# A decoder layer on one core: cheaper form of LayerNorm's column steps, modulated copies on ScalarE, the second modulation and gate both summed inside attention, and the first LayerNorm's scaling moved ahead

## The chip, the cores and the metric

The kernel runs on one core of one Trainium2 chip. Its engines are TensorE (PE: products and transposes), VectorE (DVE), ScalarE (ACT), GpSimd (POOL) and SyncE (SP, which here issues all loads and stores). The metric is device time in microseconds (us), from the first to the last instruction of one execution; lower is better.

## The reference

One transformer layer on 1024 tokens of 1024 features, all float32 with products of split operands. What is computed, cut to what matters:

```python
mod = silu(c) @ w_mod + b_mod        # shift1, scale1, gate1, shift2, scale2, gate2: 1024 each
h   = x * (1 + scale1) + shift1
q, k, v, u, iq, ik, iw = split(h @ w_in)          # 8 heads of 64, 512 pooling channels, an indexer
score = einsum(iw, relu(iq . ik)); keep the 256 best keys of each query (causal)
attn  = softmax over the kept keys (rotary q, k) @ v
pool  = (mean over the last 2/4/8/16 tokens - u) @ w_pool * pool_scale
x = layer_norm(ALPHA * x + gate1 * (concat(attn, pool) @ w_o), ln1_g, ln1_b)
h = x * (1 + scale2) + shift2
x = layer_norm(ALPHA * x + gate2 * ((silu(h @ w_gate) * (h @ w_up)) @ w_down), ln2_g, ln2_b)
```

`w_up`, `w_gate` are 1024 x 2816, `w_down` 2816 x 1024. The first LayerNorm's result is needed twice: scaled and shifted by `ln1_g`, `ln1_b` as the residual of the second, and folded with the second modulation as the feed-forward's input.

## The kernel before

Tokens are cut into eight tiles of 128, held with tokens on partitions; features are cut into eight tiles as well. Products run as three products of float32r halves (`SPLITS`), so every operand is split once into a rounded part and a rest.

The stages, with their times in the profile: first modulation, h transposed and index queries (0 to 75 us); token index scores (75 to 165); the top-256 threshold of each query, found by a search over the bits of its scores, on DVE for tiles 7, 6, 5 and on ACT and POOL for 4, 3, 2, beside the projections of u, k and v (165 to 405); attention in 32 units, a unit being a pair of heads and a query tile, later queries first (to 537); the loads and splits of the output weights with the output projection (532 to 635); residual, LayerNorm 1 and the operands of the feed-forward (575 to 660); the feed-forward, whose gate and up products are done by blocks after Winograd (635 to 1290); the last down product with LayerNorm 2 and the stores (to the end).

Instructions are recorded through `Queue` (line 121). While an engine's name is in `pinned`, its instructions keep the order in which they were written; before attention `pinned` is cleared (line 940), and from there on a scheduler may put an instruction of DVE, ACT or POOL ahead of others, as its operands allow. All instructions of engines have the helper's line, 157, in the profile, and all loads line 154, so everything below goes by the names of tiles: a buffer's name and the area of SBUF in which it lies (`modraw_V`, `stat_C`, `res_X`).

What the change touches:

- `mods()` (lines 445 to 468) makes the second modulation's scale and shift per feature: sixteen dot products of a 128x1024 block of `w_mod` (`modraw_V`, three slots in area V) with silu(c) (`srow_V`), each one DVE instruction (`CUSTOM_DVE_ANT_0 modraw_V<-modraw_V,srow_V` in the profile, followed by a row that reads its accumulator). A generator, it is stepped once per unit from unit 4 on, and its instructions may be moved by the scheduler. Its results `h2c` are first needed by `region_t`, after LayerNorm 1.
- `gate_acc` (line 426) sums a gate over eight blocks of `w_mod`, one DVE step each: a TENSOR_SCALAR, then seven SCALAR_TENSOR_TENSOR of 128x1024. It is used for the first gate at the start of the program, and for the second beside the output projection, where the sum is kept in `GR` (`gr_G`) and the blocks come through two slots of area R, three steps after each tile's LayerNorm. Two products with a matrix of ones then sum over partitions (`gt`), ACT copies them back into `GR`, and POOL adds the bias `brow`.
- `layer_norm_tile` (line 1150): statistics, then on single columns (128x1, `stat_C`) four TENSOR_SCALAR for the start of an inverse square root, and three Newton steps of two SCALAR_TENSOR_TENSOR each; in LayerNorm 1 a seventh for the shift `nm`, and ACT normalises. LayerNorm 2 (tail) calls it with `affine`: DVE or ACT and then POOL scale and shift the 1024 columns; POOL does it for all but the last tile.
- `region_t` (line 1200): transposes of a normalized tile on PE, and from their PSUM eight modulated copies of 128x128 into `stage_W`: the first four on DVE, the others on ACT.
- `affine` (line 1435): with `lnb` (gain and bias of LayerNorm 1, spread over the partitions), each residual tile is multiplied on DVE and the bias added on DVE or, for tiles 7, 5, 3, 1, on POOL; called once per block product in the first part of the feed-forward.
- `load_set`, `make_block`, `gu_step`, `down` load, build and use the blocks of feed-forward weights (`wraw`, `wblk`); `GR` is used when `make_block` scales blocks of the down weights.

## Time and profile before

| | us |
| --- | --- |
| three runs | 1356.88, 1364.34, 1357.63 (median 1357.63) |
| the profiled execution, first to last instruction | 1357.8 |
| PE busy | 1214.3 (89% of the span) |
| DVE busy | 1082.5 (80%) |
| ACT busy | 544.4 (40%) |
| POOL busy | 608.9 (45%) |
| granted clock of TensorE, mean | 0.951 of full |

The profiled execution's own time is its span, 1357.8 us, and agrees with the median of the runs. An engine's row counts the time in which it works; register, branch and DMA-issuing instructions do not count. A group of instructions of one tile is shown with its count, its busy time, and the mean duration of one; groups can overlap by a little, since an instruction may start before the one ahead has ended. The idle time before an instruction is put down to what released it last. A stretch's row shows each engine's busy time in it, and so which engine is full there, which an average over the whole span does not tell.

### The profile page before, as it was taken

What the parts mean: (1) busy time and instruction counts of PE and PEld (TensorE: products, weight loads), DVE (VectorE), ACT (ScalarE), POOL (GpSimd) and SP (SyncE); (2) the same over time, 40 slices, a digit from 0 to 9 for tenths busy, and PEclk for the clock granted to TensorE, in tenths of its full rate; (3) what the DMA queues carried; (4) which work ended last, traced back from release to release, by engine and by line L of the source; (5) the groups of instructions that cost most, each with busy time, mean ns of one, the idle gap of its engine ahead of it and who ended that gap; (6) DMA issues with size and microseconds to landing.
All of it is one profiled execution on the core that took longest, in us unless ns stands there. A gap on an engine that the chain in (4) does not pass through costs nothing.

```text
span 1357.8 us, 15982 instructions
## 1 busy us (share of the span) xinstructions
PE 1214.3 (89%) x5570; PEld 954.6 (70%) x5570; DVE 1082.5 (80%) x1763; ACT 544.4 (40%) x1019; POOL 608.9 (45%) x629
## 2 busy tenths in 40 slices
PE   7989996767849999997789999999999999999993
PEld 6646575655626666876668888888888888888872
DVE  6898899899999766499997767677676767676788
ACT  3446733553757787236422323132232313232310
POOL 1492774866534445235672415234141523423545
PEclk8989997978868999999899999999999999999997
DMA  9640020312120115520301112010110201011111
GB/s 338 232 146 16 16 93 16 124 47 78 63 70 24 55 40 192 167 76 1 109 31 63 63 41 84 32 63 32 63 63 31 94 32 62 31 63 63 63 47 77
DMA packets 24850, 101.79 MB, mean 75 GB/s; under 512 B 3393, under 2 KB 3393, under 8 KB 20290
## 3 DMA queue, kind: packets, MB, share of 16 engines
q1 hardware_dynamic: 24770, 100.77, 21.2%
q8 instruction: 44, 0.72, 0.2%
q14 instruction: 36, 0.29, 0.1%
HBM read 92.37 MB, written 8.39 MB: 74 GB/s over the span
## 4 chain that ended last, share of the span: by engine, by line
PE 50%; DVE 31%; issue 6%; POOL 5%; ACT 4%; DMA 3%; SPq 0%; DVEq 0%; POOLq 0%; ACTq 0%
PE gu L157 28%; PE dn L157 15%; DVE junk_X L157 6%; DVE stat_C L157 4%; DVE score_X L157 3%; PE s L157 2%; DVE res_X L157 2%; PE o L157 2%; PE pT L157 2%; POOL colsA_X L157 2%; DVE stage_W L157 1%; DVE colsD_X L157 1%; DVE hr_H L157 1%; DVE modraw_V L157 1%; DVE hT_H L157 1%
## 5 line engine op out<-in xcount | busy, mean ns | idle before, releaser
L157 POOL TENSOR_TENSOR wraw_R<-wraw_R 128x512 f32<-128x512 f32 x44 | 60.9, 1384 | 173.5 <-DVE wblk_T L157 52.0
L157 DVE TENSOR_TENSOR res_X<-res_X,dn 128x512 f32<-128x512 f32 (+1 forms) x145 | 97.3, 680 | 49.5 <-PE dn L157 49.5
L157 POOL TENSOR_TENSOR wraw_W<-wraw_W 128x512 f32<-128x512 f32 x44 | 60.5, 1374 | 168.5 <-DVE wblk_V L157 63.1
L157 PE MATMUL gu<-hr_H,wblk_V 128*128 128x512 f32 (+1 forms) x552 | 128.0, 387 | 8.4 <-ACT gtmp_V L157 3.7
L157 PE MATMUL pj<-ws_W,hT_H 128*128 128x512 f32 x456 | 122.1, 416 | 14.3 <-DVE kr_K L157 6.5
L157 PE MATMUL gu<-hr_H,wblk_T 128*128 128x512 f32 (+1 forms) x552 | 126.5, 386 | 4.5 <-ACT stage_W L157 4.5
L157 PE MATMUL gu<-hr_H,wblk_W 128*128 128x512 f32 (+1 forms) x552 | 124.9, 381 | 4.0 <-DVE utmp_X L157 4.0
L157 PEld LDWEIGHTS gu<-hr_H,wblk_V 128*128 128x128 f32 x552 | 102.8, 193 | 30.4 <-ACT gtmp_V L157 3.9
L157 PEld LDWEIGHTS gu<-hr_H,wblk_T 128*128 128x128 f32 x552 | 102.7, 194 | 24.5 <-ACT stage_W L157 4.8
L157 PEld LDWEIGHTS gu<-hr_H,wblk_W 128*128 128x128 f32 x552 | 100.5, 188 | 24.8 <-DVE utmp_X L157 2.8
L157 PEld LDWEIGHTS pj<-ws_W,hT_H 128*128 128x128 f32 x456 | 87.4, 198 | 41.1 <-issue 16.7
L157 DVE TENSOR_TENSOR utmp_X<-utmp_X,gu 128x512 f32<-128x512 f32 x88 | 58.1, 682 | 33.3 <-PE gu L157 32.4
L157 DVE TENSOR_TENSOR gtmp_V<-gtmp_V,gu 128x512 f32<-128x512 f32 (+1 forms) x96 | 59.4, 638 | 26.3 <-PE gu L157 26.2
L157 DVE TENSOR_SCALAR_CACHE_REDUCE junk_X<-keysD_T,colsD_X 128x1024 int16<-128x1024 int16 (+1 forms) x64 | 78.9, 1270 | 0.8
L157 POOL TENSOR_SCALAR sm_H<-sm_H,stat_X 128x1024 f32<-128x1024 f32 (+7 forms) x64 | 51.3, 816 | 62.9 <-DVE stat_X L157 47.5
L157 PE MATMUL dn<-wblk_V,act_W 128*128 128x512 f32 x288 | 75.8, 395 | 2.9 <-DVE res_X L157 2.9
L157 PE MATMUL dn<-wblk_T,act_W 128*128 128x512 f32 (+1 forms) x294 | 75.2, 385 | 2.0 <-DVE res_X L157 2.0
L157 PE MATMUL gu<-hr_H,wblk_R 128*128 128x512 f32 (+1 forms) x276 | 66.7, 391 | 4.0 <-DVE gtmp_V L157 3.4
L157 PEld LDWEIGHTS dn<-wblk_V,act_W 128*128 128x128 f32 x288 | 54.6, 190 | 15.1 <-DVE res_X L157 3.8
L157 PEld LDWEIGHTS dn<-wblk_T,act_W 128*128 128x128 f32 x294 | 54.5, 188 | 13.3 <-DVE res_X L157 2.2
L157 PEld LDWEIGHTS gu<-hr_H,wblk_R 128*128 128x128 f32 x276 | 52.0, 194 | 15.0 <-DVE gtmp_V L157 3.6
L157 PE MATMUL dn<-wblk_W,act_W 128*128 128x512 f32 x240 | 62.2, 389 | 0.0
(287 smaller groups left out, 2834.9 us busy)
## 6 DMA issues: line engine op xcount, KB each, us to landing
wm_K<-in_wma_dram SPq DMA_DIRECT2D x16, 512.0 KB, 9.8
modraw_V<-in_wmc_dram SPq DMA_DIRECT2D x16, 512.0 KB, 3.6
wraw_R<-in_wg_dram SPq DMA_DIRECT2D x6, 1024.0 KB, 4.8
wraw_R<-in_wd_dram SPq DMA_DIRECT2D x6, 1024.0 KB, 4.8
wraw_W<-in_wup_dram SPq DMA_DIRECT2D x6, 1024.0 KB, 4.7
wraw_R<-in_wup_dram SPq DMA_DIRECT2D x5, 1024.0 KB, 4.7
wraw_W<-in_wg_dram SPq DMA_DIRECT2D x5, 1024.0 KB, 4.8
wraw_W<-in_wd_dram SPq DMA_DIRECT2D x5, 1024.0 KB, 4.7
```

Of the source, the lines that this page charges most:

```text
L157: ins_ = f(*a, **k)
```

## The change

1. `mods()` starts at unit 8 and is stepped twice per unit, and its dots go through `kept`, which pins them: they stay where they were written.
2. The second gate is summed at the end of `mods()`, eight more pinned steps in area V, then summed over partitions, joined with its bias on one row and stored to `g2_d`. `GR` holds the gain of LayerNorm 1 in the meantime, and gets the gate from `g2_d` when the last residual tile has been multiplied. The steps beside the output projection, the two `gt` products and copies in the feed-forward and the bias addition on POOL are gone.
3. In `layer_norm_tile` the Newton steps and `nm` become tensor_scalar with two columns as scalars.
4. In `region_t` the first four copies are on DVE only for tiles 1 and 0, else on ACT.
5. The affine multiplications take the gain from `GR`, which is there before LayerNorm 1 ends; `lnb` holds the bias alone. `affine` is called in every second block product of the gate's second half and in five of the up's.

```diff
-MODS = (4, (0, 1, 2, 3))
+MODS = (8, 2)
...
+    g2_d = tc.dram_tile([1, 1024], F32, name="g2_d")
+    def kept(op, *a):
+        own = "V" not in pinned
+        pinned.add("V")
+        getattr(V, op)(*a)
+        if own:
+            pinned.discard("V")
...
-            V.tensor_tensor_reduce(wm, wm, srow2, 1.0, 0.0, ALU.mult, ALU.add, m2[:, u : u + 1])
+            kept("tensor_tensor_reduce", wm, wm, srow2, 1.0, 0.0, ALU.mult, ALU.add, m2[:, u : u + 1])
...
+        acc = buf("V", 4096, 1024, "gacc")
+        wms = []
+        for k in range(3):
+            wms.append(ring[(16 + k) % 3])
+            SP.dma_start(wms[k], wmg_in[1, k])
+        for k in range(KT):
+            if k == 0:
+                kept("tensor_scalar", acc, wms[k], silc[:, 0:1], None, ALU.mult)
+            else:
+                kept("scalar_tensor_tensor", acc, wms[k], silc[:, k : k + 1], acc, ALU.mult, ALU.add)
+            if k + 3 < KT:
+                wms.append(ring[(16 + k + 3) % 3])
+                SP.dma_start(wms[k + 3], wmg_in[1, k + 3])
+            yield
+        grow = buf("V", 5120, 1024, "grow")
+        SP.dma_start(grow[0:1, :], bg_in[1:2, :])
+        for c in range(2):
+            pm = psA("gt")
+            cc = slice(c * 512, (c + 1) * 512)
+            T.matmul(pm, ones, acc[:, cc], start=True, stop=True)
+            V.tensor_tensor(grow[0:1, cc], grow[0:1, cc], pm[0:1, :], ALU.add)
+        SP.dma_start(g2_d, grow[0:1, :])
...
-        if n_ >= MODS[0] and (n_ - MODS[0]) % 4 in MODS[1]:
-            next(mod_steps, None)
+        if n_ >= MODS[0]:
+            for _ in range(MODS[1]):
+                next(mod_steps, None)
...
-            V.scalar_tensor_tensor(a, y, w, y, ALU.mult, ALU.mult)
-            V.scalar_tensor_tensor(y, a, 1.5, y, ALU.add, ALU.mult)
+            V.tensor_scalar(a, y, w, y, ALU.mult, ALU.mult)
+            V.tensor_scalar(y, a, 1.5, y, ALU.add, ALU.mult)
         if affine is None:
-            V.scalar_tensor_tensor(nm, mv[:, 0:1], -1.0, y, ALU.mult, ALU.mult)
+            V.tensor_scalar(nm, mv[:, 0:1], -1.0, y, ALU.mult, ALU.mult)
...
-                if c == 0:
+                if c == 0 and t < 2:
...
-    g2 = gate_acc(1, GR, g2_ring, 1)
+    SP.dma_start(GR, ln_in[0:1, 0:1024].to_broadcast([P, 1024]))
...
-        for _ in range(3):
-            next(g2, None)
...
-    lnb = buf("W", 4096, 2048, "lnb")
-    SP.dma_start(lnb, ln_in[0:1, :].to_broadcast([P, 2048]))
+    lnb = buf("W", 5120, 1024, "lnb")
+    SP.dma_start(lnb, ln_in[0:1, 1024:2048].to_broadcast([P, 1024]))
...
-        if n == 4:
-            for c in range(2):
-                pm = psA("gt")
-                T.matmul(pm, ones, GR[:, c * 512 : (c + 1) * 512], start=True, stop=True)
-                A.activation(GR[:, c * 512 : (c + 1) * 512], pm, AF.Copy)
...
-            V.tensor_tensor(XR[t], XR[t], lnb[:, 0:1024], ALU.mult)
-            (G if t in AFF_G else V).tensor_tensor(XR[t], XR[t], lnb[:, 1024:2048], ALU.add)
+            V.tensor_tensor(XR[t], XR[t], GR, ALU.mult)
+            (G if t in AFF_G else V).tensor_tensor(XR[t], XR[t], lnb, ALU.add)
+            if not todo:
+                SP.dma_start(GR, g2_d.to_broadcast([P, 1024]))
...
-        affine()
-    G.tensor_tensor(GR, GR, brow, ALU.add)
-    gate_up("u", ACTS, lambda n: affine() if n < 4 else None)
+        if n % 2:
+            affine()
+    gate_up("u", ACTS, lambda n: affine() if n < 5 else None)
```

The built order shows where this puts instructions. On DVE in attention, `sm_H` is the masked maximum of a unit's scores `s` (one row, and one that reads its accumulator), `pT_H` a copy of transposed probabilities, `modraw_V` a dot. Before, this is where the last two of the sixteen dots stand, at the units whose key ranges are 640 and 768; fourteen are further ahead, ten of them before the first `sm_H`:

```order
L157 ISA modraw_V_3015,const_C_78<-modraw_V_3015,srow_V_3013 128x1024
L157 ISA const_C_78 128x1
L157 ISA sm_H_2588,stat_X_2583<-s_3137,score_X_77 128x640
L157 ISA stat_X_2583 128x1
L157 ISA sm_H_2588,stat_X_2583<-s_3138,score_X_77 128x640
L157 ISA stat_X_2583 128x1
L157 COPY pT_H_2587<-pT_3171 128x3x128
L157 ISA modraw_V_3014,const_C_78<-modraw_V_3014,srow_V_3013 128x1024
```

After, on DVE at the next unit with 640 keys, the first three of the sixteen:

```order
L157 ISA modraw_V_3221,const_C_78<-modraw_V_3221,srow_V_3220 128x1024
L157 ISA const_C_78 128x1
L157 ISA sm_H_2589,stat_X_2584<-s_3231,score_X_77 128x640
L157 ISA stat_X_2584 128x1
L157 ISA sm_H_2589,stat_X_2584<-s_3232,score_X_77 128x640
L157 ISA stat_X_2584 128x1
L157 COPY pT_H_2586<-pT_3263 128x128
L157 ISA modraw_V_3222,const_C_78<-modraw_V_3222,srow_V_3220 128x1024
L157 ISA const_C_78 128x1
L157 RECIPROCAL stat_X_2584<-stat_X_2584 128x2
L157 ISA modraw_V_3223,const_C_78<-modraw_V_3223,srow_V_3220 128x1024
```

All sixteen now stand here and behind, two for each unit's pair of maxima, and the eight gate steps (`gacc_V`) follow them.

On DVE at the start of LayerNorm 1, before, the last split of pooled channels (`hr_H`), four gate steps through slots of area R, and the first residuals `res_X`:

```order
L157 TENSOR_TENSOR hr_H_2676<-raw_R_75,hr_H_2676 128x3x256
L157 TENSOR_SCALAR gr_G_76<-raw_R_74,const_C_78 128x1024
L157 SCALAR_TENSOR_TENSOR gr_G_76<-raw_R_73,const_C_78,gr_G_76 128x1024
L157 SCALAR_TENSOR_TENSOR gr_G_76<-raw_R_74,const_C_78,gr_G_76 128x1024
L157 SCALAR_TENSOR_TENSOR gr_G_76<-raw_R_73,const_C_78,gr_G_76 128x1024
L157 SCALAR_TENSOR_TENSOR res_X_4053<-res_X_4053,wo_4087 128x512 x2
L157 SCALAR_TENSOR_TENSOR res_X_4052<-res_X_4052,wo_4088 128x512
```

After, at the same place on DVE:

```order
L157 TENSOR_TENSOR hr_H_2677<-raw_R_75,hr_H_2677 128x3x256
L157 TENSOR_TENSOR wblk_R_4094<-wraw_R_4101,wblk_R_4094 128x512
L157 SCALAR_TENSOR_TENSOR res_X_4080<-res_X_4080,wo_4114 128x512 x2
L157 BN_STATS stat_C_4089<-res_X_4080 128x6
L157 SCALAR_TENSOR_TENSOR res_X_4079<-res_X_4079,wo_4115 128x512
```

The gate steps are gone, and the rest of the first block of feed-forward weights, whose load is the first behind those of the pooled channels and of the gain, stands ahead of the residuals.

On SP late in attention, after, loads of the second gate's blocks (`in_wmg`) among loads of output weights (`in_wo`) and of x:

```order
L154 DMA modraw_V_3222<-in_wmg_dram 128x1024
L154 DMA raw_R_74<-in_wo_dram 128x1024
L154 DMA modraw_V_3223<-in_wmg_dram 128x1024
L154 DMA modraw_V_3221<-in_wmg_dram 128x1024
L154 DMA modraw_V_3222<-in_wmg_dram 128x1024
L154 DMA res_X_4078<-in_x_dram 128x1024
L154 DMA modraw_V_3223<-in_wmg_dram 128x1024
```

Before, no load of the second gate stands in attention; on SP they follow the last loads of output weights and pooled channels (`pool_d`), ahead of the feed-forward's first weights; here the first five of the eight:

```order
L154 DMA raw_R_74<-in_wo_dram 128x1024
L154 DMA raw_R_75<-pool_d 128x1024
L154 DMA raw_R_73<-in_wmg_dram 128x1024
L154 DMA raw_R_74<-in_wmg_dram 128x1024 x2
L154 DMA raw_R_73<-in_wmg_dram 128x1024
L154 DMA raw_R_74<-in_wmg_dram 128x1024
```

Eight loads of 512 KB have moved from behind attention into it, two of them behind a load whose target is still in use by attention.

## Rows read from the trace of the kernel before

**Rows 1.** The page: first the line of its part 1 (busy time, share of the span and number of instructions of each engine), then the first line of its part 4 (the chain of work that ended last, by engine).

```profile
PE 1214.3 (89%) x5570; PEld 954.6 (70%) x5570; DVE 1082.5 (80%) x1763; ACT 544.4 (40%) x1019; POOL 608.9 (45%) x629
...
PE 50%; DVE 31%; issue 6%; POOL 5%; ACT 4%; DMA 3%; SPq 0%; DVEq 0%; POOLq 0%; ACTq 0%
```

**Rows 2.** The view of stretches: from and to in us, length, busy time (number of instructions) of PE, PEld, DVE, ACT and POOL, then the granted clock of TensorE, the share of the DMA engines and GB/s. In order: search beside the k projection, the end of the search and the first attention units, attention up to unit 8, attention units 8 to 24, LayerNorm 1, start of the feed-forward, feed-forward, tail.

```profile
290.00:330.00 40.00, 24.36 (x88) 19.27 (x88) 38.99 (x62) 13.53 (x26) 19.08 (x23) 0.79 0.24 79
365.00:405.00 40.00, 21.08 (x86) 15.70 (x84) 39.56 (x83) 22.96 (x50) 19.63 (x48) 0.73 0.26 85
405.00:441.00 36.00, 34.41 (x178) 21.67 (x179) 33.74 (x72) 26.47 (x49) 15.39 (x16) 0.82 0.07 23
441.00:515.00 74.00, 72.63 (x510) 49.66 (x508) 51.86 (x134) 60.06 (x137) 34.96 (x37) 1.00 0.18 56
575.00:640.00 65.00, 59.42 (x294) 48.52 (x292) 61.50 (x158) 29.46 (x55) 26.48 (x18) 1.00 0.13 47
640.00:717.00 77.00, 56.71 (x274) 47.26 (x274) 74.13 (x91) 28.45 (x55) 51.71 (x29) 0.87 0.18 62
717.00:1290.00 573.00, 572.58 (x2525) 473.46 (x2523) 402.29 (x533) 164.12 (x276) 200.14 (x147) 1.00 0.16 56
1290.00:1358.00 68.00, 43.45 (x191) 35.34 (x191) 60.08 (x134) 7.47 (x6) 33.17 (x14) 0.86 0.15 62
```

**Rows 3.** Groups of DVE by tile, 290 to 403 us (before the first masked score of attention): name of the group, count, busy us and mean ns of one, idle time before them; then a row of the timeline of PE (start, duration, engine, in brackets the wait ahead of it and what ended it).

```profile
L157 DVE CUSTOM_DVE_ANT_0 modraw_V<-modraw_V,srow_V 128x1024 f32<-128x1024 f32 x10 | 13.1, 1310 | 0.0
...
401.13 2.46 PE L157 MATMUL s<-kr_K,qab_H 64*128 64x512 f32 x4 [10.98 <-DVE qab_H L157]
```

**Rows 4.** Groups of DVE by tile, 403 to 536 us (attention): the dot products, the split of output weights; a row of the DMA part of the page (loads of modulation weights: count, KB each, median us from issue to landing); timeline of DVE, two steps of the first gate.

```profile
L157 DVE CUSTOM_DVE_ANT_0 modraw_V<-modraw_V,srow_V 128x1024 f32<-128x1024 f32 x6 | 8.4, 1396 | 0.0
L157 DVE TENSOR_TENSOR wo_V<-raw_R,wo_V 128x1024 fp32r<-128x1024 f32 x2 | 3.1, 1537 | 0.0
...
modraw_V<-in_wmc_dram SPq DMA_DIRECT2D x16, 512.0 KB, 3.6
...
85.11 2.30 DVE L157 SCALAR_TENSOR_TENSOR modacc_X<-modraw_V,const_C,modacc_X 128x1024 f32<-128x1024 f32 x1
109.67 1.28 DVE L157 SCALAR_TENSOR_TENSOR modacc_X<-modraw_T,const_C,modacc_X 128x1024 f32<-128x1024 f32 x1
```

**Rows 5.** Timeline of DVE from 563 us, the first step of the second gate and the first residual of LayerNorm 1; then a row of the DMA part of the page (loads of feed-forward weights).

```profile
567.32 0.75 DVE L157 TENSOR_SCALAR gr_G<-raw_R,const_C 128x1024 f32<-128x1024 f32 x1 [2.27 <-DMA raw_R<-in_wmg_dram]
575.36 3.67 DVE L157 SCALAR_TENSOR_TENSOR res_X<-res_X,wo 128x512 f32<-128x512 f32 x6
...
wraw_R<-in_wg_dram SPq DMA_DIRECT2D x6, 1024.0 KB, 4.8
```

**Rows 6.** Groups of DVE by tile, 575 to 640 us, and the last one of ACT in the same stretch.

```profile
L157 DVE SCALAR_TENSOR_TENSOR stat_C<-stat_C 128x1 f32<-128x1 f32 x49 | 11.6, 251 | 0.9
L157 DVE TENSOR_SCALAR stage_W<-xT,const_C 128x128 f32<-128x128 f32 x24 | 8.1, 404 | 0.0
L157 DVE SCALAR_TENSOR_TENSOR gr_G<-raw_R,const_C,gr_G 128x1024 f32<-128x1024 f32 x5 | 6.4, 1280 | 2.5 <-DMA raw_R<-in_wmg_dram 2.5
L157 DVE TENSOR_SCALAR stat_C<-stat_C 128x1 f32<-128x1 f32 (+1 forms) x28 | 3.4, 148 | 0.3
...
L157 ACT ACTIVATE stage_W<-xT,const_C 128x128 f32<-128x128 f32 x24 | 8.8, 456 | 0.0
```

**Rows 7.** Groups of DVE and of POOL by tile, 640 to 717 us; and a row of the timeline of DVE there.

```profile
L157 DVE TENSOR_TENSOR res_X<-res_X,lnb_W 128x1024 f32<-128x1024 f32 x12 | 19.4, 1623 | 0.0
...
L157 POOL TENSOR_TENSOR gr_G<-gr_G,brow_W 128x1024 f32<-128x1024 f32 x1 | 3.3, 3319 | 0.0
...
680.92 1.21 DVE L157 TENSOR_TENSOR res_X<-res_X,lnb_W 128x1024 f32<-128x1024 f32 x1
```

**Rows 8.** The tail. Timeline of DVE for one token tile and the last tile, with the two groups of the column steps over 1290 to 1358 us ahead; then a row of POOL (in brackets its wait), what PE waited for in that stretch (us in total, times, longest), and its last products.

```profile
L157 DVE SCALAR_TENSOR_TENSOR stat_C<-stat_C 128x1 f32<-128x1 f32 x54 | 26.5, 491 | 1.3
L157 DVE TENSOR_SCALAR stat_C<-stat_C 128x1 f32<-128x1 f32 (+1 forms) x32 | 4.0, 149 | 0.6
...
1307.75 0.53 DVE L157 TENSOR_SCALAR stat_C<-stat_C 128x1 f32<-128x1 f32 x4
1308.31 4.08 DVE L157 SCALAR_TENSOR_TENSOR stat_C<-stat_C 128x1 f32<-128x1 f32 x3
1313.63 0.59 DVE L157 SCALAR_TENSOR_TENSOR stat_C<-stat_C 128x1 f32<-128x1 f32 x3
1346.38 0.42 DVE L157 TENSOR_TENSOR res_X<-res_X,dn 128x256 f32<-128x256 f32 x1
...
1307.50 4.87 POOL L157 TENSOR_TENSOR res_X<-res_X,wraw_R 128x1024 f32<-128x1024 f32 x2 [3.21 <-ACT res_X L157]
...
PE dn L157 <- DVE res_X L157: 4.9, 3, 2.3
...
1338.35 0.52 PE L157 MATMUL dn<-hr_H 128*128 128x256 f32 x3
```

**Rows 9.** Timeline of DVE and POOL in the search: a step of three columns, and what POOL did at that time.

```profile
302.00 1.25 DVE L157 TENSOR_SCALAR colsD_X<-colsD_X 128x3 f32<-128x3 f32 x1
...
301.06 2.16 POOL L157 TENSOR_TENSOR rope_V<-rope_V,gr_G 128x512 f32<-128x512 f32 x1
```

More of the change, by code (lines that the diff above doesn't have):

```diff
@@ L1356, in act_op @@
         return q[t % 2][:, o : o + P]
-    n_g = [0]
-    def g2_ring():
-        n_g[0] += 1
-        return RAW[n_g[0] % 2]
     first = {}
@@ L1404, in decoder_layer_kernel @@
             make_block()
-    for _ in g2:
-        pass
     for _ in range(4):
@@ L1430, in decoder_layer_kernel @@
     load_set(2)
-    brow = buf("W", 2048, 1024, "brow")
-    SP.dma_start(brow, bg_in[1:2, :].to_broadcast([P, 1024]))
     todo = list(ORDER)
```

## The prediction

> **What bounds the kernel now.** I read the page first, for who is busy and who ends the chain: PE is busy for 89% of the span, DVE for 80%, but the chain of work that ended last runs through PE for 50% and through DVE for 31% [rows 1]. So neither figure alone says what an edit is worth, and the view of stretches comes next [rows 2]. It splits the program in two kinds. In the feed-forward, 717 to 1290 us, PE is busy 572.58 of 573 us and DVE 402.29: nothing that DVE saves there counts, and work pushed into it is free. Everywhere that this change touches, DVE is the full engine: 38.99 of 40 us and 39.56 of 40 us in the search, 33.74 of 36 in the first part of attention, 61.50 of 65 in LayerNorm 1, 74.13 of 77 at the start of the feed-forward, 60.08 of 68 in the tail. The one exception is attention from unit 8 on, 441 to 515 us: PE 72.63 of 74, DVE 51.86. The change takes DVE work out of the full stretches and puts some of it into that exception. I then read the groups by tile for the size of each piece, and the timelines for what waits.
>
> **A, the search: ten dot products go.** Before, ten of the sixteen `modraw_V` dots of the second modulation run ahead of attention: 10 x 1.310 = 13.1 us on a DVE without gaps [rows 2, 3]. PE is busy there 24.36 and 21.08 of 40 us, and enters attention's scores after a wait of 10.98 us on DVE [rows 2, 3]. Nothing else is late by as much, so nearly all of it should come back; ACT and POOL search tiles 4 to 2 beside it and could hold back a part. Bounds -6 (half, if their search ends last) and -13.1; I take **-11**. Their loads leave this stretch too; its DMA engines are a quarter busy, so I give that nothing.
>
> **B, attention: sixteen dots and eight gate steps come.** One dot leaves 405 to 441 us, five leave 441 to 515, and all sixteen now stand in the latter: net 11 x 1.396 = 15.4 us [rows 4]. The gate adds one step of 0.75 [rows 5] and seven of 1.28 = 9.7 us; one split of output weights that stood here, 1.5 [rows 4], moves behind it. So DVE has 51.86 + 15.4 + 9.7 - 1.5 = 75.4 us of work in a stretch of 74 that PE fills as well. Two engines that wait for each other do not both run at 100%: between 405 and 441 us DVE reached 33.74/36 = 94% [rows 2]. At that share 75.4 us take 80.2, or +6. A gate step beside POOL took 2.30 instead of 1.28 in the first gate [rows 4]; three of seven such cost another 3. I take **+9**, with +1.4 (perfect packing) and +23.6 (all of it in series: 15.4 + 9.7 - 1.5) as ends. The pinned steps also wait for loads, and what is queued behind such a wait on DVE are the masked maxima of the next unit, on which POOL, ACT and PE wait in turn. On SP, two gate loads stand behind a load of x or of output weights that must wait for attention itself. A load lands in 3.6 us [rows 4], a slot of the three comes back every three steps, so 24 steps need 24/3 x (3.6 + 1.4) = 40 us, less than the 74 there are. I count no wait for loads, but keep it in the upper end.
>
> **C, D, E, LayerNorm 1 and the start of the feed-forward.** These are one stretch, since DVE is behind in all of it. C: the first residual starts at 575.36, behind gate steps of which the first waited 2.27 us until 567.32 [rows 5]. In the new order one split of a gate block stands there, whose load of 1024 KB takes 4.8 us [rows 5]; begun at 565.0, where that wait began, and with a copy and a split behind it (an estimate: half of 1.28 each, the gate step of twice the width), it ends near 571.1: DVE starts **4** us earlier. The LayerNorm gain, 512 KB, is issued ahead of that load on SP; where the two share the DMA engines, half of 4.8 us of this is lost again. D: off DVE go the gate steps, 4 x 1.28 = 5.1, the twenty-four modulated copies, 8.1, and of 49 column steps the difference between 251 and 148 ns, 5.0; on come six multiplications at 1.21, 7.3 [rows 6, 7]: **-10.9**. The copies land on ACT, 24 x 0.456 = 10.9 us [rows 6] on an engine busy 29.46 of 65: covered, and if that cover were gone they would cost no more than the 8.1 they save. E: of twelve 1024-wide affine steps, 19.4 us at a mean of 1.62, six are gone [rows 7]: **-9.7**. The addition on POOL (3.32 us) and the two gate copies on ACT go as well; they were beside. Together DVE has some 25 us less of the 142 between 575 and 717: 135.6 of work become 115.0, less than PE's 59.42 + 56.71 = 116.1. So PE is late next, and the gain is not 25. If PE works at the 91% that it has now in LayerNorm 1 (59.42/65), its 116.1 us take 127: **-15**. Ends: -5.6, what PE idles there between 575 and 640, and -25.9, no gap at all.
>
> **F, the tail.** Column steps of one token tile: four TENSOR_SCALAR take 0.53 us at 1307.75 while POOL is in its two multiply-adds (1307.50, 4.87 us); the three SCALAR_TENSOR_TENSOR right behind take 4.08, and three such after POOL is done 0.59 [rows 8]. So one form waits until POOL's instruction ends and the other does not. Over the tail 54 column steps take 26.5 us at 491 ns; at 149 ns, the TENSOR_SCALAR's, they are 8.0: 18.5 us off DVE, whose 60.08 become 41.6 beside PE's 43.45 [rows 2, 8]. PE is next. It waits 4.9 us for DVE's additions, and DVE adds the last piece at 1346.38, some 7.5 us behind PE's last products (1338.35 + 0.52) [rows 8]. If DVE keeps up, 4.9 and nearly all of 7.5 go: **-12**, with -14 as end where the clock (0.86 here) rises as PE's gaps close, and 0 as the other.
> That page of the Trainium skill which speaks of this port, "SBUF — State Buffer", section "Who interferes with whom", says that a DVE instruction with two SBUF inputs contends with a GpSimd one that reads SBUF; by that rule the 4.08 us are the lock, and the trace agrees.
>
> **Sum.** -11 + 9 - 15 - 12 = -29 on a profiled span of 1357.8 us, which is the median of the runs (1357.63): about **1329 us**.
>
> **Rivals.** (1) *The new form waits for POOL as well.* For it: a TENSOR_SCALAR of three columns took 1.25 us at 302.00, inside an instruction of POOL that ran from 301.06 to 303.22 [rows 9]. Against: the four single columns at 1307.75 do not wait, and single columns are what the change writes, though with two pointers for scalars, which those four have not. Then F is 0, and LayerNorm 1, with 5.0 more on DVE and so 120 against PE's 116, loses about 3: 1329 + 12 + 3 = 1344.
> The Trainium skill's "VectorE: DVE Perf Modes", section "The perf-mode tier table (the rule you actually need)", lets float32 tensor_scalar run in a 2x mode in SBUF, and "SBUF — State Buffer", section "Who interferes with whom", says that such modes take the port that GpSimd uses; by these this rival would win, and only the three-column row agrees with it.
> (2) *Attention becomes DVE's.* All that is added lies in series with PE's transposes: B is +23.6, 1329 + 14.6 = 1344. For it: 75.4 us of work in 74. Against: DVE idles 22 us there now. (3) *PE bounds LayerNorm 1.* Its products are as long as before, and only its 5.6 us of gaps up to 640 close: 1329 + 9.4 = 1338. Against: 20 us of gaps from 640 to 717, behind a late DVE. (4) *Slower: the clock falls in attention.* From 441 to 515 us it is granted 1.00; in the two search stretches where PE waits for DVE it was 0.79 and 0.73 [rows 2]. If pinned steps, held by late loads, leave PE such gaps, its 72.63 us take longer: at 0.73 they take 99, which is +25 instead of +9 (1345); the time passes 1364 once the stretch loses 44, that is 72.63/118 = a mean clock of 0.62, below any row shown; at 0.55 it would take 132, and the kernel 1378. What would have to be so for it: most units waiting for a load.
>
> **How the numbers follow.** Forecast 0.50 (1320 to 1337); rival 1 0.13; rival 2 0.13; rival 3 0.12; better than the forecast, with C to E near -25.9, 0.06; rival 4 0.06. Of the mass of rivals 1 and 2, 7 in 100 are both at once, 1358. The range takes rivals 1 to 3 in and a part of the better case: 1312 to 1347. Faster by over 0.5% (about what a measurement of this kernel can tell from no change: 6.8 us), which is below 1351: forecast, better case and most of rivals 1 to 3, 0.87. Within: both rivals at once, or rival 4 at a middling clock, 0.08. Slower: 0.05.
>
> **What would show it.** A: no dot ahead of the first masked score, which starts some 11 us earlier. B: between the same units DVE above 93%, PE's waits on DVE there a few us, clock still 1.00; waits of DVE on modulation loads would speak for rival 4. C to E: first residual near 571 less what A and B leave, PE over 90% up to the steady part. F: three column steps in 0.5 us while POOL runs, a tile every 5 to 6 us instead of 8.1, PE without waits on DVE. If column steps of 2 us remain beside POOL, rival 1 holds. I am wrong as a whole if attention gives back more than 38 us, all that the other parts gain (11 + 15 + 12).

## The result, and the profile after

The changed kernel takes 1339.22 us (median of four runs, 1337.46 to 1342.38) beside 1359.32 for the kernel before on the same chip: the ratio is 0.9856, with a 95% interval of 0.9838 to 0.9874. It is some 20 us faster. The forecast was 1329: the sign held, and the gain is two thirds of what the sum said. The time lies inside the wide range (1312 to 1347), but outside the 1320 to 1337 that had a chance of 0.50. The profiled execution spans 1340.4 us; it is the longest of the four, so the events below add up to 17.9 us and not to 20.

To see where the difference arises, I read the same events in the timelines of both kernels. The table is worked out from their rows: each number is the time of an event in the changed kernel less the time of the same event before.

| event | before, us | after, us | difference | the part of it that arose since the event above | forecast |
| --- | --- | --- | --- | --- | --- |
| first masked maximum on DVE | 403.77 | 397.39 | -6.4 | A: -6.4 | -11 |
| end of attention's last product (`o`) | 536.66 | 553.64 | +17.0 | B: +23.4 | +9 |
| first down product (`dn`) | 728.58 | 725.36 | -3.2 | C to E: -20.2 | -15 |
| end of the last DVE instruction | 1354.69 | 1336.76 | -17.9 | F: -14.7 | -12 |

The forecasts are the terms of the prediction's sum. Two of the three gains went further than the sum had them, A less far, and attention took back 23.4 us instead of 9.

The view of stretches of the changed kernel, in the columns of [rows 2] and at mostly the same times (an event now lies up to 17 us later or earlier in them):

```profile
365.00:405.00 40.00, 23.28 (x75) 16.00 (x76) 37.12 (x75) 22.22 (x47) 11.36 (x30) 0.71 0.07 20
441.00:515.00 74.00, 69.31 (x463) 45.38 (x464) 59.81 (x141) 55.33 (x125) 34.27 (x31) 1.00 0.44 147
515.00:575.00 60.00, 53.57 (x271) 38.08 (x272) 37.83 (x89) 31.78 (x83) 26.30 (x28) 0.89 0.54 187
575.00:640.00 65.00, 64.43 (x309) 53.63 (x308) 47.93 (x131) 33.05 (x67) 24.30 (x17) 1.00 0.08 26
640.00:717.00 77.00, 64.11 (x342) 56.32 (x340) 63.91 (x93) 34.19 (x69) 48.77 (x29) 0.91 0.17 59
1290.00:1340.00 50.00, 38.30 (x181) 32.01 (x179) 42.29 (x131) 7.47 (x6) 33.87 (x14) 0.91 0.21 84
```

LayerNorm 1 has changed its bound: PE is busy 64.43 of 65 us where it was 59.42, and DVE 47.93 where it was 61.50 [rows 2]. The stretch that does not fit is attention: DVE is busy 59.81 of 74 us, not full at all, and yet the end is late. A share of 81% would have passed as slack. What the share hides is seen with shorter stretches (same columns), which also show the granted clock falling; first the changed kernel, then the kernel before in its last units:

```profile
515.00:520.00 5.00, 4.47 (x22) 2.90 (x22) 4.92 (x9) 1.46 (x5) 4.46 (x3) 0.66 0.88 310
520.00:525.00 5.00, 1.19 (x4) 0.67 (x4) 5.00 (x11) 2.70 (x8) 1.36 (x2) 0.68 0.41 157
525.00:530.00 5.00, 4.12 (x7) 1.98 (x8) 3.52 (x9) 2.06 (x6) 1.15 (x2) 0.50 0.82 315
530.00:535.00 5.00, 5.00 (x32) 3.45 (x31) 1.72 (x5) 3.61 (x7) 0.94 (x2) 0.79 0.39 111
535.00:540.00 5.00, 4.75 (x38) 3.50 (x37) 4.58 (x18) 4.46 (x16) 3.53 (x2) 1.00 0.84 316
...
500.00:520.00 20.00, 18.59 (x140) 12.94 (x136) 12.02 (x36) 17.87 (x47) 12.22 (x14) 1.00 0.37 130
520.00:537.00 17.00, 16.27 (x109) 10.56 (x109) 10.10 (x47) 12.86 (x50) 12.20 (x18) 1.00 0.54 193
```

From 520 to 525 us PE does 1.19 us of work in five, and DVE is full. The clock is granted 0.66 from 515 us on and 0.50, the lower of the two levels (1.2 GHz), from 525 to 530; in the kernel before it stays at 1.00 to the end of attention. The timelines of DVE and PE in the same place (start, duration, engine; in brackets the wait and what ended it):

```profile
517.37 1.54 DVE L157 SCALAR_TENSOR_TENSOR gacc_V<-modraw_V,const_C,gacc_V 128x1024 f32<-128x1024 f32 x1
518.94 0.69 DVE L157 CUSTOM_DVE_ANT_0 sm_H<-s,score_X 128x512 f32<-128x512 f32 x1
519.56 1.44 DVE L157 SCALAR_TENSOR_TENSOR gacc_V<-modraw_V,const_C,gacc_V 128x1024 f32<-128x1024 f32 x1
520.92 0.68 DVE L157 CUSTOM_DVE_ANT_0 sm_H<-s,score_X 128x512 f32<-128x512 f32 x1
521.53 1.27 DVE L157 SCALAR_TENSOR_TENSOR gacc_V<-modraw_V,const_C,gacc_V 128x1024 f32<-128x1024 f32 x1
524.07 1.66 DVE L157 SCALAR_TENSOR_TENSOR gacc_V<-modraw_V,const_C,gacc_V 128x1024 f32<-128x1024 f32 x1
...
521.66 1.19 PE L157 MATMUL s<-kr_K,qab_X 128*128 128x256 f32 x4 [2.19 <-DVE stat_X L157]
525.88 3.75 PE L157 MATMUL gt<-gacc_V,const_C 128*128 128x512 f32 x4 [3.04 <-DVE stat_X L157]
```

A gate step of 1.54 and then 1.44 us stands ahead of each of the two maxima of 0.69 and 0.68 us, and two more, of 1.27 and 1.66 us, follow. PE waits 2.19 us for a unit's maximum, then 3.04 at the gate's two products over partitions (one row), which stand in PE's own order and need the last gate step (it ends at 525.73); they take 3.75 us, at the lower clock.

The tail shows what was foreseen. Groups and timeline of DVE, then POOL:

```profile
L157 DVE TENSOR_SCALAR stat_C<-stat_C 128x1 f32<-128x1 f32 (+1 forms) x86 | 16.6, 204 | 1.9
...
1308.12 1.39 DVE L157 TENSOR_SCALAR stat_C<-stat_C 128x1 f32<-128x1 f32 x7
1310.75 0.76 DVE L157 TENSOR_SCALAR stat_C<-stat_C 128x1 f32<-128x1 f32 x3
1313.56 1.47 DVE L157 TENSOR_SCALAR stat_C<-stat_C 128x1 f32<-128x1 f32 x7
1329.79 0.41 DVE L157 TENSOR_TENSOR res_X<-res_X,dn 128x256 f32<-128x256 f32 x1
...
1307.43 4.87 POOL L157 TENSOR_TENSOR res_X<-res_X,wraw_R 128x1024 f32<-128x1024 f32 x2 [0.57 <-ACT res_X L157]
```

Seven column steps take 1.39 us in the midst of POOL's 4.87, where three took 4.08 [rows 8]. A tile comes every 5.44 us (1308.12, 1313.56) instead of 8.1; this is PE's own pace, since no wait of PE is left in the tail. All 86 column steps together are now 16.6 us instead of 26.5 + 4.0 [rows 8].

### The profile page after: what moved, and what is told of

Its sections match the earlier page's. It is cut to its first block, busy times and chain, and to the rows that moved or that the text cites. A ratio compares the mean times of both kernels' runs of the same rounds, so it can differ in the third digit from the quotient of the medians.

```text
span 1340.4 us, 15983 instructions
## 1 busy us (share of the span) xinstructions
PE 1218.3 (91%) x5570; PEld 958.0 (71%) x5570; DVE 1045.4 (78%) x1741; ACT 551.4 (41%) x1041; POOL 602.1 (45%) x628
## 5 line engine op out<-in xcount | busy, mean ns | idle before, releaser
L157 PE MATMUL pj<-ws_W,hT_H 128*128 128x512 f32 x456 | 124.8, 423 | 18.7 <-DVE kr_K L157 6.5
L157 POOL TENSOR_SCALAR sm_H<-sm_H,stat_X 128x1024 f32<-128x1024 f32 (+7 forms) x64 | 58.7, 931 | 70.4 <-DVE stat_X L157 57.3
L157 DVE TENSOR_TENSOR utmp_X<-utmp_X,gu 128x512 f32<-128x512 f32 x88 | 58.2, 682 | 33.5 <-PE gu L157 32.4
L157 ACT ACTIVATE act_W<-gtmp_V 128x512 fp32r<-128x512 f32 x40 | 25.3, 633 | 95.0 <-DVE gtmp_V L157 92.9
L157 PEld LDWEIGHTS dn<-wblk_V,act_W 128*128 128x128 f32 x288 | 54.1, 188 | 11.2
```

Source lines behind the costliest of these rows:

```text
L157: ins_ = f(*a, **k)
```

## The experiments

Each kernel was timed in rounds beside the kernel before (medians of 1357.73, 1359.79 and 1358.61 in the three groups, in the order below: four kernels each). A difference from the changed kernel is one of medians from different groups; by the ratios it comes out up to 2 us otherwise. "Later" and "earlier" are from the timelines, against the kernel before; a unit's time is the start of the reciprocal of its sums on DVE.

**1. The column steps alone**, in the kernel before.

```diff
-            V.scalar_tensor_tensor(a, y, w, y, ALU.mult, ALU.mult)
-            V.scalar_tensor_tensor(y, a, 1.5, y, ALU.add, ALU.mult)
+            V.tensor_scalar(a, y, w, y, ALU.mult, ALU.mult)
+            V.tensor_scalar(y, a, 1.5, y, ALU.add, ALU.mult)
```

> The kernel before with the column steps of both LayerNorms as tensor_scalar, and nothing else of the change. If the old form waits for POOL and the new one does not (my theory), the tail gives all that the changed kernel gained there, 14.7 us, and LayerNorm 1 some 2 to 5 more beside the work that it keeps: 1338 to 1344 against 1359. If the tail's gain in the changed kernel came from an earlier or lighter stretch ahead of it (rival), the tail stays within 4 us of before: 1355 or more.

Measured: 1344.67 us, ratio 0.9907 (0.9890 to 0.9924), 13 us less. In its trace the first down product is 4.7 us earlier and the end 19.4, so the tail alone gives 14.7, as much as in the changed kernel. This one edit is two thirds of the whole gain.

**2. The old column steps**, in the changed kernel (the edit above, reversed).

> The changed kernel with the column steps back in the old form. My theory: the tail is as before, one tile every 8 us, and LayerNorm 1 loses a few us: 1354 to 1360. The rival, by which the other parts made the tail shorter: 1340 to 1345.

Measured: 1355.42 us, ratio 0.9981 (0.9968 to 0.9993). The tail is that of before to 0.01 us: first down product 5.45 us earlier, end 5.45 earlier. The group of column steps reads as in [rows 8]:

```profile
L157 DVE SCALAR_TENSOR_TENSOR stat_C<-stat_C 128x1 f32<-128x1 f32 x54 | 26.5, 490 | 1.3
```

With 1, this settles F: the form of these steps is the whole gain of the tail, and without it the change is worth 2 us.

**3. The second gate left out.**

```diff
-            SP.dma_start(wms[k], wmg_in[1, k])
...
-                kept("scalar_tensor_tensor", acc, wms[k], silc[:, k : k + 1], acc, ALU.mult, ALU.add)
...
-            T.matmul(pm, ones, acc[:, cc], start=True, stop=True)
-            V.tensor_tensor(grow[0:1, cc], grow[0:1, cc], pm[0:1, :], ALU.add)
```

> The changed kernel without the second gate's eight loads, eight steps and two products in attention (the gate is its bias alone: that part of the computation is left out). Theory, that these steps stand in series with the maxima of units 19 to 25, where 13 us are lost: attention ends 10 to 14 us earlier, 1325 to 1330. Rival, that the dots are what costs and the gate hides behind PE: 1335 to 1340.

Measured: 1328.18 us, ratio 0.9791 (0.9775 to 0.9806): 11 us less than the changed kernel. By the ratios it is 9 us. Attention ends 12.6 us earlier than there (541.05), and the clock stays at 1.00 from 441 us to its end; its last stretch:

```profile
515.00:541.00 26.00, 24.11 (x159) 15.47 (x157) 16.30 (x64) 21.76 (x70) 20.05 (x24) 1.00 0.64 224
```

From the first maximum to its end attention still takes 10.8 us more than before. So the dots alone already cost a little more than the 9 us that the sum had for dots and gate, and the gate doubles it.

**4. The gate's two products behind attention**, the sum kept in another area; `gate_end` holds the products, the additions and the store.

```diff
-        acc = buf("V", 4096, 1024, "gacc")
+        acc = buf("T", 0, 1024, "gacc")
...
     pair_cat(0, 3, pair_pv(0, 3))
+    gate_end()
```

> The changed kernel with the gate's sum kept in another area and its two products over partitions, with the additions and the store, written behind the last attention unit, so that PE's queue does not wait there for the last gate step. If those products are the main part of the loss (PE waits 3.0 us for the last step, they take 3.75 us, and the clock is at 0.59 around them): 1331 to 1334. If the steps on DVE are the loss: 1336 to 1340.

Measured: 1341.44 us, ratio 0.9882 (0.9864 to 0.9899). Nothing is gained: PE no longer waits at these products (they run at 554.3 us), but the steps alone still hold up the units, and the clock is granted 0.69 from 515 to 520 us and 0.66 from 525 to 535. PE's longest wait there is for POOL's part of a unit, which itself waited 5.31 us for DVE:

```profile
527.23 1.11 PE L157 MATMUL pT<-const_C,sm_H 128*128 128x128 f32 x4 [3.50 <-POOL sm_H L157]
...
515.00:520.00 5.00, 3.74 (x20) 2.59 (x21) 4.96 (x9) 2.28 (x6) 4.17 (x3) 0.69 0.88 313
```

So the products' place among the late units is not needed for the loss.

**5. All added steps narrow**: the dots and gate steps on 8 columns, with every load and slot kept. One instruction is added, which clears the sum (`MEMSET`, 0.91 us at 499.50).

```diff
-            kept("tensor_tensor_reduce", wm, wm, srow2, 1.0, 0.0, ALU.mult, ALU.add, m2[:, u : u + 1])
+            kept("tensor_tensor_reduce", wm[:, 0:8], wm[:, 0:8], srow2[:, 0:8], 1.0, 0.0, ALU.mult, ALU.add, m2[:, u : u + 1])
-                kept("tensor_scalar", acc, wms[k], silc[:, 0:1], None, ALU.mult)
+                V.memset(acc, 0.0)
+                kept("tensor_scalar", acc[:, 0:8], wms[k][:, 0:8], silc[:, 0:1], None, ALU.mult)
...
-                kept("scalar_tensor_tensor", acc, wms[k], silc[:, k : k + 1], acc, ALU.mult, ALU.add)
+                kept("scalar_tensor_tensor", acc[:, 0:8], wms[k][:, 0:8], silc[:, k : k + 1], acc[:, 0:8], ALU.mult, ALU.add)
```

> The changed kernel in which the sixteen dots and the eight gate steps work on 8 columns of each block instead of 1024 (the rest of these sums is left out); every load, slot and wait stays. If attention's loss is the time of these steps on DVE, in series with the maxima: it ends 20 us earlier or more, near 532, and the whole is 1314 to 1322. If the loss is in the waits (loads late, their issue held on SP, the pinned places): 1333 to 1340.

Measured: 1329.68 us, ratio 0.9779 (0.9763 to 0.9796), between what either theory said. Up to unit 24 the first did hold: the unit's sums are 4.4 us earlier than before, where the changed kernel has them 11.4 later, so up to there the loss comes with the width of the steps. Then 10.8 us are lost with hardly any DVE time added (6.4 later at unit 31). The timeline of DVE and PE of this kernel, and two stretches:

```profile
511.60 0.36 DVE L157 SCALAR_TENSOR_TENSOR gacc_V<-modraw_V,const_C,gacc_V 128x8 f32<-128x8 f32 x1
513.03 0.22 DVE L157 SCALAR_TENSOR_TENSOR gacc_V<-modraw_V,const_C,gacc_V 128x8 f32<-128x8 f32 x1
...
513.39 3.31 PE L157 MATMUL gt<-gacc_V,const_C 128*128 128x512 f32 x4 [2.07 <-DVE gacc_V L157]
530.03 0.89 PE L157 MATMUL pT<-const_C,sm_H 128*128 128x128 f32 x4 [1.44 <-POOL sm_H L157]
...
500.00:520.00 20.00, 17.93 (x106) 11.53 (x105) 13.45 (x49) 14.93 (x40) 9.41 (x13) 0.91 0.81 251
520.00:540.00 20.00, 17.88 (x96) 12.39 (x96) 11.14 (x46) 14.04 (x47) 13.70 (x15) 0.77 0.63 223
```

Here PE comes to the products before the last narrow step is done and waits 2.07 us in its own order; with the 3.31 us that the products take, this is 5.4 of the 10.8 us. Later PE waits 1.44 us for POOL, and the clock is at 0.77 from 520 to 540 us. So products that wait for the last step are a second way to lose time, beside steps between the late units' maxima (experiment 4); that they alone bring all of the 10.8 us is not shown.

**6. Nothing pinned.**

```diff
     def kept(op, *a):
-        own = "V" not in pinned
-        pinned.add("V")
         getattr(V, op)(*a)
-        if own:
-            pinned.discard("V")
```

> The changed kernel with the dots and gate steps not pinned: in its order ten dots stand in the search again, as before, and the others ahead of unit 12; the gate steps stay in the last third. If taking the dots out of the search brought less (6.4 us at the first maximum) than their new place costs: attention ends 3 to 6 us earlier than in the changed kernel, 1333 to 1337. If the move itself is worth its price: 1340 to 1346.

Measured: 1330.03 us, ratio 0.9782 (0.9763 to 0.9801): 9 us less than the changed kernel, and better than either expectation. Ten dots are back in the search, and the first maximum is 2.3 us later than before; but the slots of area V come free sooner, and the gate is summed between 465 and 483 us, beside units with 640 and 768 keys. The whole of it costs attention 3.2 us (2.3 later at its start, 5.5 at its end). The timeline of DVE, first and last gate steps, and of PE, the two products, then stretches:

```profile
465.81 1.27 DVE L157 SCALAR_TENSOR_TENSOR gacc_V<-modraw_V,const_C,gacc_V 128x1024 f32<-128x1024 f32 x1
481.72 1.28 DVE L157 SCALAR_TENSOR_TENSOR gacc_V<-modraw_V,const_C,gacc_V 128x1024 f32<-128x1024 f32 x1
...
517.23 1.96 PE L157 MATMUL gt<-gacc_V,const_C 128*128 128x512 f32 x4 [0.26 <-DVE qab_X L157]
...
460.00:480.00 20.00, 19.23 (x132) 12.76 (x132) 18.37 (x39) 13.04 (x29) 9.32 (x9) 1.00 0.58 186
500.00:520.00 20.00, 19.74 (x134) 12.91 (x133) 13.04 (x42) 17.51 (x46) 9.88 (x13) 1.00 0.16 53
520.00:540.00 20.00, 18.44 (x129) 12.14 (x128) 13.72 (x55) 16.82 (x57) 15.57 (x21) 1.00 0.75 264
```

DVE is at 92% from 460 to 480 us and PE still at 96%, at full clock. PE hardly waits there for the steps that make it wait forty microseconds later in the changed kernel. The two products run at 517.23 us (525.88 in the changed kernel); they wait 0.26 us, and take 1.96 at full clock.

**7. One step per unit from unit 2 on.**

```diff
-MODS = (8, 2)
+MODS = (2, 1)
```

> The changed kernel with one step per unit from unit 2 on instead of two from unit 8 on, still pinned. If the loss comes from two steps of 1.2 us ahead of one unit's maxima, which PE's slack of two units does not cover, while one would be covered: 1328 to 1333. If each step costs its time wherever it is: 1338 to 1342.

Measured: 1344.66 us, ratio 0.9892 (0.9875 to 0.9908), 5 us worse than the changed kernel; both expectations missed. The dots are cheaper so (0.8 us later than before at unit 18, where the changed kernel is 5.0 later), but the gate comes later still, from 511 to 538 us, and the units from 25 to 31 lose 10 us (1.1 later at unit 25, 11.2 at unit 31), with the clock at 0.79 from 520 to 560 us. Even so attention ends 5.5 us earlier than in the changed kernel (548.17). The 5 us come from behind it: from there to the first down product it takes 179.7 us against 171.7, of which 6.2 lie ahead of the first residual. In that part, here and then in the changed kernel, PE is busy:

```profile
548.17:587.86 39.69, 34.86 (x140) 27.60 (x140) 19.79 (x18) 12.60 (x17) 11.95 (x5) 0.91 0.45 147
...
553.64:587.09 33.45, 32.88 (x144) 26.86 (x145) 15.27 (x17) 11.44 (x16) 7.18 (x3) 1.00 0.49 157
```

PE's longest wait is 2.4 us, for a rounded block of output weights from ACT; what made it late was not tried.

**8. The modulated copies back on DVE.**

```diff
-                if c == 0 and t < 2:
+                if c == 0:
```

> The changed kernel with the first four modulated copies of every tile on DVE again. If PE bounds LayerNorm 1 by now, as the stretch after the change says (64.43 of 65 us busy), these 8 us of DVE cost little: 1339 to 1342. If DVE still sets the pace: 1344 to 1348.

Measured: 1343.23 us, ratio 0.9879 (0.9862 to 0.9897), 4 us more than the changed kernel, with intervals that overlap. The trace says the same: from the end of attention to the first down product it takes 174.7 us against 171.7. DVE has 60.59 us of work in a stretch of 63 again, and PE 61.51:

```profile
586.00:649.00 63.00, 61.51 (x308) 51.37 (x307) 60.59 (x158) 29.30 (x53) 31.30 (x19) 1.00 0.00 1
```

So 8 us off DVE are worth about 3 in LayerNorm 1.

**9 and 10. Only the gate free, and only the dots free.**

The first has the gate's steps unpinned,

```diff
-                kept("scalar_tensor_tensor", acc, wms[k], silc[:, k : k + 1], acc, ALU.mult, ALU.add)
+                V.scalar_tensor_tensor(acc, wms[k], silc[:, k : k + 1], acc, ALU.mult, ALU.add)
```

the second the dots.

```diff
-            kept("tensor_tensor_reduce", wm, wm, srow2, 1.0, 0.0, ALU.mult, ALU.add, m2[:, u : u + 1])
+            V.tensor_tensor_reduce(wm, wm, srow2, 1.0, 0.0, ALU.mult, ALU.add, m2[:, u : u + 1])
```

> The changed kernel with the sixteen dots pinned as in the change and only the eight gate steps not pinned. The trace of the kernel with nothing pinned has no fall of the clock in attention and is 9 us faster. If the pinned gate steps cause the fall (PE's gaps at units 19 to 25, clock 0.50 to 0.79 for 20 us): attention ends 5 to 8 us earlier, 1331 to 1335. If the pinned dots, two ahead of one unit, are what costs: 1338 to 1341.

> The changed kernel with the gate steps pinned and the dots not. By the first reading (pinned gate steps make the clock fall) it keeps the loss of the last units: 1336 to 1341. By the other (the dots are the cost, 9 us from unit 12 to 19): 1329 to 1333.

Measured: 1340.61 us, ratio 0.9865 (0.9849 to 0.9880), and 1337.64 us, ratio 0.9837 (0.9821 to 0.9852). Neither alone does what both do. With the gate free, its steps still come late, since its blocks wait for slots that pinned dots hold. With the dots free, all but one of the gate steps stay where they were written, in the late units (3.0 us later than before at unit 18, 13.4 at unit 25), with the clock at 0.83 from 520 to 540 us. It is not the pin that costs, but where the steps come to stand.

**11. One dot per unit, pinned, then a free gate.**

```diff
-MODS = (8, 2)
+MODS = (2, 18)
...
-            for _ in range(MODS[1]):
+            for _ in range(1 if n_ < MODS[1] else 2):
```

with the gate as in 9.

> Dots pinned, one per unit from unit 2 to 17, then the gate not pinned, two steps per unit. In the trace with one step per unit the units up to 18 were 2 us earlier than before, and the loss came after unit 24 with the clock. If a free gate removes that fall: attention ends at 538 to 541, and the whole is 1324 to 1329. If the clock falls all the same: 1337 to 1345.

Measured: 1338.84 us, ratio 0.9853 (0.9839 to 0.9867). 1.4 us later at unit 18 and 12.7 at unit 25: the clock is at 0.73 from 520 to 540 us. Cheaper dots do not help a late gate.

**12. Nothing pinned, and the first block's split on POOL.**

```diff
-        split(dst, src, 512)
+        split(dst, src, 512, G if pos["made"] == 1 else V)
```

> The kernel with nothing pinned, and the split of the first block of feed-forward weights on POOL, so that the first residual does not stand behind it on DVE (there it waits 5.68 us for the load and ACT, and PE later 5.2 us for the first normalized tile). If that wait sets the end: 3 to 5 us less than with nothing pinned, 1325 to 1327. If PE, full from 575 to 634 us, takes the wait elsewhere: 1329 to 1331.

Measured: 1326.98 us, ratio 0.9771 (0.9757 to 0.9785). In the changed kernel the first residual stands behind this split, which waits for ACT and its load:

```profile
586.48 0.69 DVE L157 TENSOR_TENSOR wblk_R<-wraw_R,wblk_R 128x512 fp32r<-128x512 f32 x1 [4.65 <-ACT wblk_R L157]
587.09 1.28 DVE L157 SCALAR_TENSOR_TENSOR res_X<-res_X,wo 128x512 f32<-128x512 f32 x2
```

and here it doesn't:

```profile
569.82 1.29 DVE L157 SCALAR_TENSOR_TENSOR res_X<-res_X,wo 128x512 f32<-128x512 f32 x2 [1.29 <-PE wo L157]
```

From the end of attention to the first residual it takes 29.5 us, with nothing pinned 33.5, and to the first down product 169.5 instead of 172.1. The medians differ by 3 us and the ratios by 1.5, which is within the two intervals; the traces' 2.6 point the same way, so a gain of some 2 us is likely, not shown. This is the fastest kernel of the study, 12 us under the changed one.

## Why the prediction was right in sign, and its gain too large

The terms missed by +4.6 (A), +14.4 (B), -5.2 (C to E) and -2.7 us (F). That the time still lies in the wide range is in part luck: what C to E and F gave beyond the sum paid for 7.9 of the 19.0 that A and B fell short.

**A was mis-sized: -6.4 instead of -11.** The ten dots are gone from the search, but the scheduler moved the end of tile 5's search ahead of the first maximum, and beyond that the early units are not DVE's. With all sixteen dots gone up to unit 8, DVE is busy 27.82 of the 36 us from 405 to 441, where it was 33.74:

```profile
405.00:441.00 36.00, 32.44 (x178) 20.84 (x177) 27.82 (x57) 22.99 (x46) 15.72 (x19) 0.85 0.03 8
```

and unit 11 is only 4.2 us earlier than before. PE, busy 32.44 of 36 us at a granted clock of 0.85, looks like the next bound; no run tests that. The prediction named DVE as full there and did not ask what a unit takes on PE.

**B is the step that failed: "at that share 75.4 us take 80.2".** The work was counted rightly: sixteen dots take 20.4 us and eight gate steps 10.7 in the trace of after. What was wrong is the pricing of 74 us as one stretch with one busy share. It holds two kinds of units. Up to unit 18 a step displaces a maximum, and the thirteen dots between units 11 and 18 turn 4.2 us earlier into 5.0 later: 9.2 us, a little over half of what the steps take (13 x 1.28 = 16.6 us). Narrow steps (experiment 5) lose next to nothing there, 0.7 us. That is not DVE's time alone: beside the wide steps POOL's part of a unit takes longer too. Its groups by shape from 441 to 540 us, for units of 512 keys, before, in the changed kernel and with narrow steps:

```profile
L157 POOL TENSOR_SCALAR sm_H<-sm_H,stat_X 128x512 f32<-128x512 f32 x8 | 5.5, 696 | 2.5 <-DVE stat_X L157 2.5
...
L157 POOL TENSOR_SCALAR sm_H<-sm_H,stat_X 128x512 f32<-128x512 f32 x8 | 8.2, 1036 | 10.6 <-DVE stat_X L157 10.6
...
L157 POOL TENSOR_SCALAR sm_H<-sm_H,stat_X 128x512 f32<-128x512 f32 x8 | 5.4, 693 | 6.5 <-DVE stat_X L157 4.4 <-DVE gacc_V L157 2.1
```

No run keeps one of the two and takes away the other, so their shares are open. From unit 16 on the maxima are short (512 and 384 keys, from unit 24 on 256 and 128). Beside these the gate's steps let PE wait: 11 us from unit 18 to 25 (5.0 later, then 16.0), with the clock falling in between. That PE has less of other units' work to turn to there is argued, not shown. Rival 2 put the price at +23.6, everything in series, and +23.4 is what came, but not by its mechanism: the dots cost a little over half of their time, and the gate's 11 us hold the products and the lower clock as well, so the agreement is chance. Rival 4's mechanism was part of it, with PE's gaps from the steps and the products instead of from loads: DVE never waited for a modulation load, as the prediction had counted. The one thing it did not price at all are the two products in PE's order, 1.96 us at full clock (experiment 6) and 3.75 here.

**C to E: -20.2 for -15.** PE became the bound, as said (64.43 of 65). It also gained in the stretch behind, where it is busy 64.11 of 77 us instead of 56.71: the sum held it to the 91% of [rows 2] and it reached 99% up to 640 us. The copies back on DVE cost 3 to 4 us of this (experiment 8). The column steps bring 4.7 alone (experiment 1), but nothing in the changed kernel, where PE sets the pace: with the old ones (experiment 2) the stretch takes 171.1 us, with the new 171.7. The point on C failed by its reason: 4 us earlier came true as 5.0 (from the end of the last split of pooled channels, 581.83, to 587.09 are 5.3 us, where it was 10.3 from the start of the gate's first wait to 575.36), but the split of the first block waited 4.65 in it; whether the gain's load ahead of its own is to blame was not tried.

**F: -14.7 for -12.** Mechanism and place as said, and both experiments on it agree. The price of a step was too low: 149 ns is the TENSOR_SCALAR with immediates, and with two columns as scalars it takes some 236 (below). So 13.9 us came off DVE instead of 18.5, which cost nothing, since PE sets the pace. PE has no wait on DVE's additions left, and the lag of 7.5 us has gone to 1.5 (last product ends 1328.30, last addition starts 1329.79).
By the Trainium skill's "SBUF — State Buffer", section "Who interferes with whom", the old form's second input in SBUF is what contends with GpSimd; the runs agree, since the form is all that changed in experiment 1. What the Trainium skill's "VectorE: DVE Perf Modes", section "The perf-mode tier table (the rule you actually need)", says of a 2x mode for tensor_scalar, by which rival 1 would have won, does not show on single columns in any run here.

Rival 1 is out: 1.39 us for seven steps inside POOL's 4.87. Rival 3 is out: PE's gaps from 640 to 717 us shrank as well, from 20 to 13 us.

**What stays open.** In experiment 5 the units behind the products lose more than the wait of 2.07 us; the lower clock is in the rows, but how much of the 10.8 us is its own beyond the wait and the products' 3.31 us, and whether loads of x and of output weights that stand behind the gate's have a part, was not tried. Nor was a version that takes the dots out of the search and has the gate early as well, two steps per unit from unit 2.

## What to carry to other kernels

Price work that is added to a stretch by the units in it, not by the stretch's busy share: in this kernel a step cost little over half its time, or less, beside a long unit that keeps PE full, and its time or more, with PE's clock falling, beside a short one. The same gate cost some 3 us with its steps at 465 to 483 us (dots where they were before), and 9 to 13 with them at 508 to 526. Where small column operations run beside POOL, look at how long the same form takes with POOL and without; a rewrite from a two-tensor form to a scalar form was two thirds of this gain. And an ordered queue that comes to its work before another engine's last step is done stands idle until then (the products on PE: 3.04 us in the changed kernel, 2.07 in experiment 5). Moving the products alone gained nothing here (experiment 4), since the steps held up the units as well.

## What the runs showed of the hardware that was not expected

A tensor_scalar on one column with two columns as scalars takes longer than with immediates. The 86 column steps of the tail take 204 ns in the mean; 32 of them have immediates, at 149 ns as before, which leaves some 236 for the other 54 (an estimate from these rows: 86 x 204 less 32 x 149, over 54). So the new form is not shorter by itself: three take 0.76 us (1310.75 above, still inside POOL's 4.87), three of the old form 0.59 where POOL is done [rows 8]. Its whole use is that it does not wait for POOL. On three columns the same instruction with float32 did wait [rows 9]; on one column the longest in the changed kernel's tail takes 0.27 us.

The clock fell to its lower level twice in attention's late units (changed kernel, same columns):

```profile
505.00:515.00 10.00, 7.52 (x49) 4.63 (x48) 8.98 (x22) 8.02 (x20) 5.69 (x6) 1.00 0.59 201
515.00:518.40 3.40, 3.40 (x16) 2.44 (x18) 3.35 (x6) 0.96 (x3) 2.94 (x2) 0.50 0.88 319
518.40:521.80 3.40, 1.21 (x10) 0.60 (x7) 3.37 (x7) 1.24 (x4) 1.53 (x2) 1.00 0.84 298
521.80:532.10 10.30, 7.26 (x19) 4.16 (x20) 7.73 (x18) 4.79 (x13) 2.86 (x5) 0.50 0.46 178
532.10:545.00 12.90, 11.76 (x84) 7.66 (x82) 7.10 (x28) 10.23 (x31) 9.12 (x12) 1.00 0.59 205
...
514.91 1.03 PE L157 MATMUL pT<-const_C,sm_H 128*128 128x128 f32 x4 [1.44 <-ACT pT_H L157]
```

The first fall, at 515.0, comes ahead of the waits of 2.19 and 3.04 us; PE had waited 1.44 us for ACT just before it (last row). The second, at 521.8, comes right behind the wait of 2.19 us, and the wait of 3.04 lies inside it. The clock came back at 532.1; PE had been busy without a gap from 530 on. Where no wait of PE was longer than 0.7 us (nothing pinned, 515 to 545), it stayed at 1.00.
